# The first 36 microseconds of a two-layer decoder: loads reordered, the first gain spread by TensorE, and the engines' order written by hand

## Chip, cores and metric

The kernel runs on one NeuronCore of a Trainium2 chip, as one program. The metric is the device time of a run in microseconds, lower is better. Engines are called by their common names: TensorE (PE, with its weight loads as PEld), VectorE (DVE), ScalarE (ACT), GpSimd (POOL) and SyncE (SP), which here only issues loads.

## What is computed

Two layers over 512 tokens of 1024 features. Only the first step of the first layer matters here: a norm with a gain, and the projection to 416 "latent" columns (256 for queries, 128 for keys and values, 32 rotary) and to the other heads' queries, keys and values.

```python
def rms_norm(x, g):
    xf = x.astype(jnp.float32)
    y = xf * lax.rsqrt(jnp.mean(xf * xf, axis=-1, keepdims=True) + NORM_EPS)
    return (y * g.astype(jnp.float32)).astype(x.dtype)

h = rms_norm(x, ev_pre_g[0])
c_q, c_kv, k_rope, dq, dk, dv = split_cols(h @ ev_w_in[0], EVEN_SPLITS)   # 256, 128, 32, 512, 512, 512
q = heads_first(rms_norm(c_q, cq_g) @ w_uq, MLA_HEADS)
kv = heads_first(rms_norm(c_kv, ckv_g) @ w_ukv, MLA_HEADS)
```

## The kernel before

The 512 tokens are four tiles `X[i]` of 128 partitions by 1024, handled in the order 3, 2, 1, 0 (`ORDER`). Matrix products are done in three parts with split operands: a float32 value is cast to a shorter form `h` on ACT, DVE takes the remainder `l = x - h`, and TensorE adds `h*h`, `h*l` and `l*h` (`mm3`, lines 263 to 265). The class `Weights` does this for weights: `load` issues a load into one of three `wraw` buffers, `split` (lines 72 and 73) casts to `wh` and subtracts to `wl`, and `ahead(n)` sees that n units are made. A load into a `wraw` buffer waits until the split that read it is done. All loads go through SP's queue in program order.

At the start TensorE multiplies a tile of zeros 16 times (`warm`, line 137). The gain `ev_pre_g` is loaded with its row repeated into all 128 partitions. For each token tile, `normalise` computes the mean square on ACT (`Square`, line 188), the reciprocal root on POOL (lines 178 and 181), the product with the gain on DVE in two halves (`xn`, line 201), then four TensorE transposes into a bank of PSUM for each half (`tp`, line 211), a cast on ACT (`xh`, line 171) and the remainder on DVE (`xl`, line 172). Between the tiles one more of the four weight units of the latent projection is made (`W.ahead`). The latent projection `ac` follows for each tile: 8 blocks of 128 features with three products each, 416 columns wide, so 24 products a tile and 96 in all; then the latent norm (`ctok`) and its transposes (`tc`). After that the products of the first differential head (`aqk`, 512 wide) begin.

PSUM has eight banks; `bank("a", ...)` hands out three of them in turn. The order of the instructions on each engine is chosen by the scheduler of the language from the program order and its own costs, except in blocks under `tc.manual_schedule`, where the written order holds for the engines it names.

Of the kernel before, what the change touches and what calls it, by code (L numbers as in the profile page):

```python
# [9 lines left out]
F32 = mybir.dt.float32  # L10
# [3 lines left out]
ALU = mybir.AluOpType  # L14
# [3 lines left out]
P = 128  # L18
S = 512
D = 1024  # L20
NT = S // P
KD = D // P
EPS = 1e-6
# [2 lines left out]
NF = FF // P  # L26
HF = NF // 2
LAM_INIT = 0.8 - 0.6 * math.exp(0.0)
WARM = 16
TURN = 4  # L30
ORDER = (3, 2, 1, 0)

# [54 lines left out]
def trunk(tc, A, out):  # L87
    nc = tc.nc
    PE, ACT, DVE, POOL = nc.tensor, nc.scalar, nc.vector, nc.gpsimd

    with ExitStack() as top:
# [36 lines left out]
        def load_x(i):  # L128
            nc.sync.dma_start(X[i][:], A["x"][i * P:(i + 1) * P, :])

        load_x(3)

        zero = chp.tile([P, P], F32, tag="s", name="zero")
        DVE.memset(zero[:], 0.0)
        warm = bank("o", "warm")
        for _ in range(WARM):
            PE.matmul(warm[:, :P], zero[:], zero[:], start=True, stop=True)
        POOL.memset(epst[:], EPS)
        POOL.memset(mhalf[:], -0.5)
# [411 lines left out]
        def even():  # L551
            with ExitStack() as es:
# [3 lines left out]
                dv = ap.tile([P, NT, 512], F32, tag="dv", name="dv")  # L556
                oM = (ap.tile([P, 4, S], F32R, tag="omh", name="omh"),
                      ap.tile([P, 4, S], F32R, tag="oml", name="oml"))
                g_pre = gain("ev_pre_g", 0)
                nc.sync.dma_start(ident[:], A["ident"])  # L560
                for n, i in enumerate(ORDER[1:]):
                    W.load()
                    load_x(i)
                xnT = new_xnT()
                xh, xl = xnT

# [24 lines left out]
                with ExitStack() as e1:  # L591
# [19 lines left out]
                    with ExitStack() as e2:  # L611
# [10 lines left out]
                        nc.sync.dma_start(qtab[:], A["rope_q"])  # L622
                        for i in ORDER:
                            t = slice(i * P, (i + 1) * P)
                            a = bank("a", "ac")
                            for k in range(KD):
# [750 lines left out]
```

## Time and profile before

| | us |
|---|---|
| median of 3 runs | 1167.95 (1167.81 to 1168.21) |
| the profiled execution | 1168.91 |
| its span | 1167.1 |
| TensorE busy | 1145.5, 98% of the span |
| DVE busy | 810.8, 69% |
| ACT busy | 558.2, 48% |

A row of the timeline gives the start in microseconds from the start of the span, the duration, the engine, the source line, the operation, what it writes and reads by the program's names, the shape, how many instructions are merged in it, and in brackets how long the engine was idle before it and what ended that. Products on TensorE are pipelined: the next one starts before the one before it has ended, so the distance between starts is the cost of one. A row of the stretches gives each engine's busy time with the number of instructions, the granted TensorE clock (1.00 is full), the busy share of the DMA engines and the rate.

### The profile page before, as it was taken

To read this page: it belongs to the slowest core of one execution; us is meant where nothing else is said; L and a number is where in the kernel's file an instruction comes from. 1 tells how busy PE (TensorE), PEld (TensorE's weight loads), DVE (VectorE), ACT (ScalarE), POOL (GpSimd) and SP (SyncE) were. 2 spreads that over 40 slices of the span, in tenths; PEclk is the share of its full clock that TensorE was granted. 3 is DMA by queue.
4 is the path that set the end of the run, shared out by engine and by line. 5 is a ranking of instruction groups with operands and counts; after the bars stand their busy time and mean duration, and the time that the engine had idled before them with its cause. 6 is when DMAs were issued, how large, how long until landed. Compare 5 with 4: busy or idle time off the path is not lost. (4 is left out here: it accounts for less than half of the span.)

```text
span 1167.1 us, 15181 instructions
## 1 busy us (share of the span) xinstructions
PE 1145.5 (98%) x5656; PEld 939.4 (80%) x5656; DVE 810.8 (69%) x1424; ACT 558.2 (48%) x942; POOL 57.4 (5%) x138
## 2 busy tenths in 40 slices
PE   8999999999999999999999999999999999999997
PEld 7876667898888888888878877898988888888885
DVE  6677676457766767899863465666676766779896
ACT  5565555245443443457543454544444443445562
POOL 2100012110000000000020000002000000000001
PEclk9999999999999999999999999999999999999999
DMA  8310521043323322355735212322333333324461
GB/s 283 114 63 1 169 73 38 37 138 120 108 91 93 106 90 89 110 154 163 234 114 152 72 55 90 91 74 86 96 112 90 107 92 93 106 81 140 141 207 72
DMA packets 39049, 126.81 MB, mean 109 GB/s; under 512 B 4672, under 2 KB 6336, under 8 KB 38848
## 3 DMA queue, kind: packets, MB, share of 16 engines
q1 hardware_dynamic: 37056, 122.11, 33.6%
q10 hardware_dynamic: 1920, 3.74, 1.1%
q8 instruction: 44, 0.72, 0.3%
q14 instruction: 29, 0.24, 0.1%
HBM read 117.95 MB, written 6.29 MB: 106 GB/s over the span
## 5 line engine op out<-in xcount | busy, mean ns | idle before, releaser
L73 DVE TENSOR_TENSOR wl<-wraw,wh 128x1024 fp32r<-128x1024 f32 (+1 forms) x202 | 244.5, 1218 | 186.2 <-ACT wh L72 185.8
L72 ACT CAST wh<-wraw 128x1024 fp32r<-128x1024 f32 (+1 forms) x202 | 209.7, 1047 | 282.2 <-PE u L264 179.4
L264 PE MATMUL u<-xl,wh 128*128 128x512 f32 (+1 forms) x768 | 285.3, 372 | 0.1
L265 PE MATMUL u<-xh,wl 128*128 128x512 f32 (+1 forms) x768 | 285.2, 372 | 0.0
L263 PE MATMUL u<-xh,wh 128*128 128x512 f32 (+1 forms) x768 | 285.0, 372 | 0.1
L264 PEld LDWEIGHTS u<-xl,wh 128*128 128x128 f32 x768 | 144.6, 188 | 25.3 <-DVE xl L172 0.3
L263 PEld LDWEIGHTS u<-xh,wh 128*128 128x128 f32 x768 | 144.4, 188 | 25.3 <-ACT xh L171 0.6
L265 PEld LDWEIGHTS u<-xh,wl 128*128 128x128 f32 x768 | 144.6, 188 | 25.0
L264 PE MATMUL acc<-wl,gh 128*128 128x512 f32 x248 | 96.5, 389 | 0.0
L265 PE MATMUL acc<-wh,gl 128*128 128x512 f32 x248 | 96.5, 389 | 0.0
L263 PE MATMUL acc<-wh,gh 128*128 128x512 f32 x248 | 96.4, 390 | 0.0
L412 ACT ACTIVATE y<-u,cw 128x512 f32<-128x512 f32 x88 | 67.5, 775 | 1.8 <-PE u L265 1.8
L417 ACT ACTIVATE y<-y 128x512 f32<-128x512 f32 x44 | 27.7, 632 | 85.0 <-DVE y L415 85.0
L415 DVE SCALAR_TENSOR_TENSOR y<-u,cw,y 128x510 f32<-128x510 f32 x88 | 65.6, 747 | 2.5
L413 DVE SCALAR_TENSOR_TENSOR y<-u,cw,y 128x511 f32<-128x511 f32 x88 | 65.1, 744 | 0.9 <-ACT y L412 0.9
L178 POOL TENSOR_TENSOR rv<-ms,epst 128x1 f32<-128x1 f32 x40 | 11.0, 276 | 924.9 <-ACT junk L230 845.1
L263 PEld LDWEIGHTS acc<-wh,gh 128*128 128x128 f32 x248 | 46.5, 188 | 10.2 <-issue 0.5
L265 PEld LDWEIGHTS acc<-wh,gl 128*128 128x128 f32 x248 | 46.6, 188 | 9.7
L264 PEld LDWEIGHTS acc<-wl,gh 128*128 128x128 f32 x248 | 46.5, 188 | 9.6
L263 PE MATMUL apt<-xh,wh 128*128 128x512 f32 x128 | 51.3, 401 | 0.0
L265 PE MATMUL apt<-xh,wl 128*128 128x512 f32 x128 | 50.6, 395 | 0.0
L264 PE MATMUL apt<-xl,wh 128*128 128x512 f32 x128 | 50.5, 395 | 0.0
(297 smaller groups left out, 1907.2 us busy)
## 6 DMA issues: line engine op xcount, KB each, us to landing
wraw<-in_ffn_w_up SPq DMA_DIRECT2D x88, 512.0 KB, 3.6
wraw<-in_ffn_w_down SPq DMA_DIRECT2D x44, 512.0 KB, 3.7
wraw<-in_od_w_dqk SPq DMA_DIRECT2D x12, 512.0 KB, 3.6
wraw<-in_ffn_w_down SPq DMA_DIRECT2D x22, 256.0 KB, 2.7
wraw<-in_ev_w_dqk SPq DMA_DIRECT2D x8, 512.0 KB, 3.6
wraw<-in_ev_w_out SPq DMA_DIRECT2D x8, 512.0 KB, 3.7
spill<-X SPq DMA_DIRECT2D x8, 512.0 KB, 2.6
X<-spill SPq DMA_DIRECT2D x8, 512.0 KB, 6.3
```

The source lines that it names most:

```text
L72: self.nc.scalar.copy(h[:, :w], raw[:, :w])
L73: self.nc.vector.tensor_tensor(l[:, :w], raw[:, :w], h[:, :w].bitcast(F32), ALU.subtract)
L178: POOL.tensor_tensor(v[:, :n], ms, epst[:, :n], ALU.add)
L263: PE.matmul(o, lh, rh, start=first, stop=False, skip_group_check=more)
L264: PE.matmul(o, lh, rl, start=False, stop=False, skip_group_check=more)
L265: PE.matmul(o, ll, rh, start=False, stop=last, skip_group_check=more)
L412: ACT.activation(y[:, z], u, AF.Identity, bias=c[:, 3:4], scale=c[:, 2:3])
L413: DVE.scalar_tensor_tensor(y[:, z, 1:], u[:, :S - 1], c[:, 1:2], y[:, z, 1:], ALU.mult, ALU.add)
L415: DVE.scalar_tensor_tensor(y[:, z, 2:], u[:, :S - 2], c[:, 0:1], y[:, z, 2:], ALU.mult, ALU.add)
L417: ACT.activation(y[:, 0], y[:, 0], AF.Silu)
```

## The change

The loads: the second token tile comes second on SP's queue, then the first weight unit, the identity for the transposes, the second and third weight units, the fourth into a part of `dv` (a buffer that is not used until later), then tiles 1 and 0. The gain's 4 KB row is loaded alone, into partition 0 of a zeroed tile, on ACT's queue.

The gain is spread by two float32 products of a full 128 by 128 tile of ones with that zeroed tile: each row of the result, in two PSUM banks of the tag "a", is the gain. The first two tiles' norms read it there; ACT then copies it back to `g_pre` for the last two.

The order on TensorE, DVE, ACT and POOL is written by hand from the first filler product to tile 0's norm. The fillers are 12 at first, 6 after the gain's products, and one between the two transposes of tile 3. The latent products are issued in groups by kind, and those of tile 2 are issued among those of tile 3.

```diff
-WARM = 16
+WARM = 12
...
-        zero = chp.tile([P, P], F32, tag="s", name="zero")
-        DVE.memset(zero[:], 0.0)
-        warm = bank("o", "warm")
-        for _ in range(WARM):
-            PE.matmul(warm[:, :P], zero[:], zero[:], start=True, stop=True)
...
-                g_pre = gain("ev_pre_g", 0)
+                zero, ones = dqk[0][:, 0, :P], dqk[1][:, 0, :P]
+                POOL.memset(zero, 0.0)
+                g_pre = glob.tile([P, D], F32, tag="gain", name="gain", bufs=2)
+                DVE.memset(g_pre[:], 0.0)
+                POOL.memset(ones, 1.0)
...
+                nc.scalar.dma_start(g_pre[0:1, :], A["ev_pre_g"][0:1, :])
+                load_x(2)
+                W.load()
                 nc.sync.dma_start(ident[:], A["ident"])
-                for n, i in enumerate(ORDER[1:]):
-                    W.load()
-                    load_x(i)
+                W.load()
+                W.load()
+                raw = dv[:, 0:2].rearrange("p a b -> p (a b)")
+                nc.sync.dma_start(raw[:, :832], A["ev_w_c"][3])
+                W.raws.append(raw)
+                load_x(1)
+                load_x(0)
...
-                    for n, i in enumerate(ORDER):
-                        normalise(i, g_pre, xnT, "tn" if i % 2 else "ss")()
-                        W.ahead((2, 3, 4, 4)[n])
+                    first = tc.manual_schedule(engines={PE.engine, DVE.engine, ACT.engine, POOL.engine})
+                    first.__enter__()
...
+                    busy(WARM)
+                    gb = [bank("a", "gb") for _ in range(2)]
+                    for n in range(2):
+                        PE.matmul(gb[n], ones, g_pre[:, n * S:(n + 1) * S], start=True, stop=True)
+                    busy(6)
+                    r3, r2 = mean_square(X[3][:]), mean_square(X[2][:])
+                    xn3 = normed(3, r3, gb)
+                    W.ahead(1)
+                    columns(3, 0, xn3)()
+                    busy(1)
+                    lo = columns(3, 1, xn3)
+                    W.ahead(2)
+                    lo()
+                    W.ahead(3)
+                    xn2 = normed(2, r2, gb)
+                    W.ahead(4)
+                    r1 = mean_square(X[1][:])
...
+                    for ks in ((0, 1), (2, 3), (4, 5)):
+                        for what in ("hh", "lh", "hl") if ks[0] else ("hh", "hl", "lh"):
+                            down_part(3, what, ks)
+                    down_part(3, "hh", (6, 7))
+                    down_part(3, "lh", (6, 7))
+                    for n in range(2):
+                        columns(2, n, xn2)()
+                    for n in range(2):
+                        ACT.copy(g_pre[:, n * S:(n + 1) * S], gb[n])
+                    r0 = mean_square(X[0][:])
+                    down_part(2, "hh", range(4))
+                    down_part(2, "hl", range(4))
+                    down_part(3, "hl", (6, 7))
+                    down_part(2, "lh", range(4))
+                    down_part(2, "hh", range(4, 8))
+                    down_part(2, "hl", range(4, 8))
+                    g_sb = [g_pre[:, :S], g_pre[:, S:]]
+                    xn1 = normed(1, r1, g_sb)
+                    for n in range(2):
+                        columns(1, n, xn1)()
+                    down_part(2, "lh", range(4, 8))
+                    xn0 = normed(0, r0, g_sb)
+                    first.__exit__(None, None, None)
+                    for n in range(2):
+                        columns(0, n, xn0)()
```

`busy(n)` issues n filler products; `normed` is the DVE part of `normalise` in two halves; `columns(i, n, xn)` issues the four transposes and the cast of one half and returns the DVE remainder; `down_part(i, what, ks)` issues the latent products of one kind of tile i for the blocks `ks`, into a bank that it takes from tag "a" at the first of them.

More of the change, by code (lines that the diff above doesn't have):

```diff
@@ L131, in trunk @@
         load_x(3)
-        zero = chp.tile([P, P], F32, tag="s", name="zero")
-        DVE.memset(zero[:], 0.0)
-        warm = bank("o", "warm")
-        for _ in range(WARM):
-            PE.matmul(warm[:, :P], zero[:], zero[:], start=True, stop=True)
-        POOL.memset(epst[:], EPS)
-        POOL.memset(mhalf[:], -0.5)
         def ffn_units(layer):
@@ L558, in even @@
                       ap.tile([P, 4, S], F32R, tag="oml", name="oml"))
-                g_pre = gain("ev_pre_g", 0)
-                nc.sync.dma_start(ident[:], A["ident"])
-                for n, i in enumerate(ORDER[1:]):
-                    W.load()
-                    load_x(i)
+                zero, ones = dqk[0][:, 0, :P], dqk[1][:, 0, :P]
[3 more added lines that the diff above has]
+                POOL.memset(ones, 1.0)
+                POOL.memset(epst[:], EPS)
+                POOL.memset(mhalf[:], -0.5)
+                nc.scalar.dma_start(g_pre[0:1, :], A["ev_pre_g"][0:1, :])
+                load_x(2)
+                W.load()
+                nc.sync.dma_start(ident[:], A["ident"])
+                W.load()
[5 more added lines that the diff above has]
+                load_x(0)
                 xnT = new_xnT()
@@ L595, in even, with busy @@
                     mv = mp.tile([P, NT, 512], F32, tag="mv", name="mv")
-                    for n, i in enumerate(ORDER):
-                        normalise(i, g_pre, xnT, "tn" if i % 2 else "ss")()
-                        W.ahead((2, 3, 4, 4)[n])
+                    first = tc.manual_schedule(engines={PE.engine, DVE.engine, ACT.engine, POOL.engine})
+                    first.__enter__()
+                    warm = bank("o", "warm")
+                    def busy(n):
+                        for _ in range(n):
+                            PE.matmul(warm[:, :P], zero, zero, start=True, stop=True)
@@ new lines, in normed, with columns @@
+                    def normed(i, r, g):
+                        xn = chp.tile([P, D], F32, tag="s", name="xn")
+                        for half in range(2):
+                            c = slice(half * S, half * S + S)
+                            DVE.scalar_tensor_tensor(xn[:, c], X[i][:, c], r[:, 0:1], g[half], ALU.mult, ALU.mult)
+                        return xn
+                    def columns(i, n, xn):
+                        tp = bank(("tn" if i % 2 else "ss")[n], "tp", 4, P)
+                        for k in range(4):
+                            PE.transpose(tp[:, k], xn[:, (4 * n + k) * P:(4 * n + k + 1) * P], ident[:])
+                        d = (slice(None), slice(4 * n, 4 * n + 4), slice(i * P, (i + 1) * P))
+                        ACT.copy(xh[d], tp)
+                        return lambda: DVE.tensor_tensor(xl[d], tp, xh[d].bitcast(F32), ALU.subtract)
@@ new lines, in even, with down_part @@
+                    W.ahead(2)
[4 more added lines that the diff above has]
+                    r1 = mean_square(X[1][:])
+                    ac, done = {}, {}
+                    def down_part(i, what, ks):
+                        if i not in ac:
+                            ac[i], done[i] = bank("a", "ac"), 0
+                        t = slice(i * P, (i + 1) * P)
+                        for k in ks:
+                            c = slice((k % 2) * 416, (k % 2 + 1) * 416)
+                            done[i] += 1
+                            PE.matmul(ac[i][:, :416], (xl if what == "lh" else xh)[:, k, t],
+                                      W.made[k // 2][what == "hl"][:, c], start=done[i] == 1, stop=done[i] == 3 * KD)
@@ L624, in even @@
                             t = slice(i * P, (i + 1) * P)
-                            a = bank("a", "ac")
-                            for k in range(KD):
+                            if i not in ac:
+                                ac[i] = bank("a", "ac")
+                            a = ac[i]
+                            for k in range(KD) if i < 2 else ():
                                 wh, wl = wc[k // 2]
```

## The prediction, made before the changed kernel was run

> **What bounds the kernel now.** I read the page first, then TensorE's timeline over the first 36 us, then the clock and engine shares by stretches of 3.41 us, then ACT, DVE, POOL and the loads in the same stretch. The page:
>
> ```profile
> span 1167.1 us, 15181 instructions
> PE 1145.5 (98%) x5656; PEld 939.4 (80%) x5656; DVE 810.8 (69%) x1424; ACT 558.2 (48%) x942; POOL 57.4 (5%) x138
> ```
>
> TensorE is the bound: a change at the start is worth only what it does to the moment from which TensorE runs without a gap. TensorE's timeline (start, duration, idle before) shows that moment:
>
> ```profile
> 1.05 5.61 PE L137 MATMUL warm<-zero 128*128 128x128 f32 x32 [1.05 <-DVE zero L134]
> 7.73 1.32 PE L211 MATMUL tp<-ident,xn 128*128 128x128 f32 x8 [1.07 <-DVE xn L201]
> 11.09 0.46 PE L263 MATMUL ac<-wh,xh 128*128 128x416 f32 x1 [2.04 <-ACT xh L171]
> 12.31 1.11 PE L211 MATMUL tp<-ident,xn 128*128 128x128 f32 x4 [0.57 <-DVE xn L201]
> 16.14 0.60 PE L211 MATMUL tp<-ident,xn 128*128 128x128 f32 x4
> 16.50 0.44 PE L265 MATMUL ac<-wh,xl 128*128 128x416 f32 x1
> 16.77 0.35 PE L263 MATMUL ac<-wh,xh 128*128 128x416 f32 x1
> 16.96 0.35 PE L265 MATMUL ac<-wh,xl 128*128 128x416 f32 x1
> 35.58 0.39 PE L263 MATMUL aqk<-xh,wh 128*128 128x512 f32 x1
> ```
>
> After the fillers there are three gaps; from 16 us a product starts every 0.19 us (16.77, 16.96), and four transposes take 0.36 us and slow the next product by 0.08, so 0.44. The first `aqk` product, at 35.58, is my finish line: from there on the changed program issues TensorE's products in the same order as before but for one pair of `tc` transposes, and the other engines' orders converge soon after, so I take the difference there as the difference of the whole. The same stretches with the granted clock (the last three figures of a row: PEclk, DMA share, GB/s):
>
> ```profile
> core 0: us, PE busy (x) PEld busy (x) DVE busy (x) ACT busy (x) POOL busy (x), PEclk, DMA share, GB/s
> 1.39:4.80 3.41, 3.41 (x17) 3.41 (x17) 0.00 (x0) 0.97 (x2) 0.00 (x0) 1.00 0.87 270
> 4.80:8.22 3.42, 2.35 (x21) 2.09 (x19) 1.30 (x2) 0.91 (x3) 0.75 (x2) 1.00 0.98 323
> 8.22:11.63 3.41, 1.36 (x8) 0.72 (x6) 1.27 (x3) 2.99 (x6) 0.74 (x2) 1.00 1.03 419
> 11.63:15.04 3.41, 2.84 (x11) 2.65 (x11) 3.41 (x6) 2.26 (x5) 0.00 (x0) 0.50 0.68 275
> 653.34:656.75 3.41, 2.46 (x12) 1.82 (x11) 3.41 (x8) 1.12 (x1) 0.00 (x0) 1.00 0.75 180
> 656.75:660.16 3.41, 3.41 (x9) 2.63 (x9) 2.03 (x5) 2.08 (x2) 0.00 (x0) 0.50 0.35 132
> ```
>
> After a stretch with 1.36 us of TensorE work, the clock is 0.50 for the next 3.41 us; the same follows 2.46 us of work at 653. (The first stretch shows 1.00, but its products run at the slow pace, below.)
>
> **The change, part by part.** *Fillers and the gain.* The rows of the filler, of a float32 product 512 wide, and of what is available for the new small load:
>
> ```profile
> 3.98 0.63 PE L137 MATMUL warm<-zero 128*128 128x128 f32 x2
> 4.20 0.64 PE L137 MATMUL warm<-zero 128*128 128x128 f32 x2
> 5.94 0.50 PE L137 MATMUL warm<-zero 128*128 128x128 f32 x3
> 6.05 0.50 PE L137 MATMUL warm<-zero 128*128 128x128 f32 x3
> 73.73 0.59 PE L687 MATMUL sps<-mk,mq 128*128 128x512 f32 x1
> 73.73 1.02 PE L687 MATMUL sps<-mk,mq 128*128 128x512 f32 x2
> gain<-in_ev_pre_g SPq DMA_DIRECT2D x1, 512.0 KB, 5.6
> ident<-in_ident SPq DMA_DIRECT2D x1, 64.0 KB, 5.3
> on<-ob SPq DMA_DIRECT2D x16, 33.0 KB, 1.9
> ```
>
> A float32 product is two passes. A filler pass takes 0.21 us before 4.8 us and 0.11 after (starts 3.98, 4.20; 5.94, 6.05); a pass 512 wide takes 1.02 - 0.59 = 0.43. So 12 fillers, 24 passes from 1.1: 17 slow ones to 4.8, 7 fast ones to 5.6. The two gain products, four passes: 1.7, to 7.3. Six more fillers: 1.3, to 8.7. These stand ahead of the first transposes in TensorE's written order, so those start at 8.7, not 7.73: this part *loses* 1.0. The zeros now come from POOL; the trace has no such memset there, so I keep the start of 1.1, and a later one costs at most its own delay, half a microsecond I think.
>
> The gain row must be there by 5.6. It is issued on ACT's queue behind DVE's memset of 1024 columns, which the trace does not show; zeroing 128 columns ended at 1.0, so I take an issue at about 2. Landing takes between 1.9 (33 KB in a quiet queue) and 5.3 (ident behind two loads): 3.9 to 7.3. I take the low end's side, under 5.6, because one row on a queue of its own resembles the 1.9 more; the high end costs 1.7. ACT's table load and first Square stand behind that issue, but Square waits for X until 4.45 anyway.
>
> What the broadcast load cost is little: without it DVE could have started when r was ready.
>
> ```profile
> 4.45 1.06 ACT L188 ACTIVATE junk<-X 128x1024 bf16<-128x1024 f32 x1 [2.44 <-DMA X<-in_x]
> 8.11 0.89 ACT L72 CAST wh<-wraw 128x832 fp32r<-128x832 f32 x1 [2.51 <-DMA wraw<-in_ev_w_c]
> 10.47 1.05 ACT L171 CAST xh<-tp 128x512 fp32r<-128x512 f32 x2
> 6.02 0.56 POOL L181 TENSOR_TENSOR rr<-rv,mhalf 128x1 f32<-128x1 f32 x1
> 6.92 1.42 DVE L201 SCALAR_TENSOR_TENSOR xn<-X,rr,gain 128x512 f32<-128x512 f32 x2 [5.93 <-DMA gain<-in_ev_pre_g]
> 9.03 1.03 DVE L73 TENSOR_TENSOR wl<-wraw,wh 128x832 fp32r<-128x832 f32 x1 [0.69 <-ACT wh L72]
> 12.17 1.28 DVE L172 TENSOR_TENSOR xl<-tp,xh 128x512 fp32r<-128x512 f32 x2
> 6.00:13.00 7.00, 3.31 (x19) 2.30 (x19) 3.94 (x6) 3.78 (x6) 1.30 (x3) 0.90 1.02 411
> ```
>
> r ends at 6.58 and DVE starts at 6.92: 0.3. At the 411 GB/s of the last row, 416 KB weights land about 1 us apart; taking the 512 KB broadcast out and the fourth weight into `dv`, X2 (the second tile) lands near 6, the weights near 7, 8.3, 9.3, 10.3 (estimates). None is then waited for.
>
> *The first tiles.* After: xn3 6.7 to 8.2, transposes 8.7 to 9.9 with one filler between. ACT (orders as built): Square of X3 and X2 and cast 0 before 9; xh of the two halves 9.4 to 10.6; casts 1, 2, 3 from 10.5, 0.8 to 0.9 each, to 13.0; Square of X1 to 14.1. DVE: xl of the first half to 10.7, then wl1 only when cast 1 is done (11.5 to 12.5), the second xl to 13.1, wl2 to 14.0, xn2 to 15.4, wl3 to 16.3. TensorE follows these: tile 3's first products at 10.0, waits of 0.3 before `wh1`, 0.3 before `wl1`, 0.4 before `wl2`, the last of 22 products near 15.2, tile 2's eight transposes to 16.2. Then a new wait. Tile 2's accumulator takes the bank of the first gain product, which frees only when ACT has copied it out; that copy stands behind both xh copies of tile 2 on ACT (15.9, 16.4, then 16.9 to 17.5). So TensorE stands 1.4 and goes on at 17.5.
>
> *Where that stands against before*, by counting `tp` and `ac` work up to 17.5 (two answers, first of `ac`, then of `tp`):
>
> ```profile
> 9.50:17.50 8.00, 4.88 (x18) 4.17 (x19) 0.00 (x0) 0.00 (x0) 0.79 0.76 294
> 0.00:9.50 9.50, 1.31 (x8) 0.84 (x8) 0.00 (x0) 0.00 (x0) 1.00 0.81 270
> 9.50:17.50 8.00, 1.71 (x8) 1.22 (x8) 2.07 (x4) 2.23 (x4) 0.79 0.76 294
> 17.50:35.58 18.08, 17.89 (x106) 1.00 0.63 197
> ```
>
> Before: 18 products and 16 transposes. After: 22 and 16. The lead is 4 x 0.19 = 0.8 us. The last row says that before, TensorE had only 0.2 us idle from there to the finish line, so nothing more can be gained there. After, I find small waits: tile 1's low half behind wl4 and tile 3's latent steps on DVE (0.1), xn0 (0.1), the extra `tc` pair ahead of the line (0.3, of no worth later), and `ctok` of tile 1 (0.4, against 0.2 of before). Counting between none and all of it beyond before, 0.0 to 0.7, I take 0.4.
>
> Sum: -0.8 + 0.4 = -0.4 us. Against the profiled execution, 1168.91 us (1.8 around the span), that is 1168.5; that execution lies 0.96 over the median of 1167.95, so the median becomes 1167.5. Without the chosen middle, 1167.1 to 1167.9; with half a microsecond for the estimated landings and copies either way, 1166.6 to 1168.4.
>
> **The clock gate against the skill.** By my steps TensorE works 3.2 of the 3.41 us up to 11.63 and 3.0 up to 15.04, but only 2.2 of those from 15.04 to 18.46: between the 2.35 that the clock survived and the 1.36 that it did not, and below the 2.46 at 653 that it did not. The Trainium skill, "TensorE: Matmul & The Clock Gate", section "What's actually happening", says that the clock halves after an idle window of about 3.4 us, and that the window is free-running. By that rule no stretch of the changed start would lose its clock. The trace disagrees on the first point: its longest gap before the halving is 2.04 us.
>
> **Rivals.**
> 1. One halved stretch, at 18.46 to 21.87, where TensorE has no gap: 3.41 / 2 = 1.7 lost, 1169.2. For it: the 2.46 row. Against: the 2.35 row. Still within the bound.
> 2. Slower: the small gain load. TensorE's written order lets nothing past the gain products, so each microsecond beyond 5.6 delays everything by one. At 7.3 it is 1.7, and the gap of 1.7 then falls into the stretch that decides the clock for 8.22 to 11.63 (1.4 by my steps, since the slow transposes and products there are what all wait for). 1167.5 + 1.7 + 1.4 = 1170.6. It decides from a landing beyond about 6.5.
> 3. Faster: the written order runs without its waits. If casts and splits overlap better than I lined them up, the 0.3 + 0.3 + 0.4 + 1.4 shrink; all gone gives 1167.5 - 2.4 = 1165.1. Against: DVE has work in nearly all of 11.5 to 16.3.
> 4. The broadcast's removal does nothing: as shown it was worth 0.3 at most, and lies inside my sum.
>
> **The numbers.** Forecast 0.50; rival 1, 0.20; rival 2 or a halved stretch beside another delay, 0.17; rival 3, 0.13. A change under 0.2% (2.3 us; 1165.6 to 1170.3), about what a measurement of this kernel can tell from none, holds the first two. Rival 3 is faster (0.13), rival 2 slower (0.17). Rivals 2 and 3 hold more than 2 in 10, so the range reaches to their prices: 1165.1 to 1170.6; the forecast's own is 1166.6 to 1168.4.
>
> **What would show it.** In the profile after: the first `tp` near 8.7 behind fillers; `gb` starting at 5.6 with no wait for a load; a gap over 1 us ahead of tile 2's first `ac` product, ended by ACT's gain copy; `aqk` at 35.2, and PEclk 1.00 throughout the first 36 us. A first `aqk` before 33.2 or after 37.9 makes it wrong; so does a `gb` that waits for its load.

## Result, and the profile after

The changed kernel takes 1170.35 us (median of 22 runs, 1168.31 to 1172.37), the kernel before 1168.12 (22 runs, 1166.89 to 1170.92). The ratio is 1.0014, with a 95% interval of 1.0008 to 1.0019: 1.6 us slower (0.9 to 2.2), where 0.4 faster was forecast. The profiled execution takes 1171.49 us. Its page:

```profile
span 1169.7 us, 15206 instructions
PE 1149.1 (98%) x5666; PEld 939.9 (80%) x5666; DVE 812.2 (69%) x1424; ACT 558.4 (48%) x944; POOL 56.0 (5%) x140
```

TensorE has ten passes more (5666 for 5656), a figure that turns out to matter. TensorE's timeline of the changed kernel over the same stretch:

```profile
1.06 5.27 PE L608 MATMUL warm<-dqk 128*128 128x128 f32 x24 [1.06 <-POOL dqk L553]
6.17 1.96 PE L628 MATMUL gb<-gain,dqk 128*128 128x512 f32 x4
7.96 1.50 PE L608 MATMUL warm<-dqk 128*128 128x128 f32 x12
9.30 0.60 PE L620 MATMUL tp<-ident,xn 128*128 128x128 f32 x4
15.85 1.03 PE L620 MATMUL tp<-ident,xn 128*128 128x128 f32 x8
18.11 1.03 PE L652 MATMUL ac<-wh,xh 128*128 128x416 f32 x4 [1.22 <-ACT gain L663]
35.91 0.39 PE L254 MATMUL aqk<-xh,wh 128*128 128x512 f32 x1
```

Fillers, gain products, six more fillers, the first `tp` at 9.30 (8.7 was forecast), the gap of 1.22 that ACT's gain copy ends (1.4 at 17.5 was forecast), and the finish line at 35.91, against 35.58 before and 35.2 forecast. The clock by stretches, in the columns explained above:

```profile
8.22:11.63 3.41, 3.40 (x27) 3.10 (x26) 2.32 (x3) 1.62 (x3) 0.00 (x0) 1.00 1.04 418
11.63:15.04 3.41, 3.21 (x14) 2.14 (x13) 3.04 (x4) 2.96 (x5) 0.29 (x2) 1.00 0.70 235
15.04:18.46 3.42, 2.20 (x16) 1.91 (x15) 3.13 (x6) 1.97 (x5) 0.45 (x1) 1.00 0.87 230
657.91:661.32 3.41, 3.41 (x9) 2.64 (x10) 2.41 (x6) 1.70 (x2) 0.00 (x0) 0.50 0.46 143
```

The start keeps its clock, the stretch with 2.20 us of work included. (These stretches are cut where the clock of the execution before could change. In this execution the clock rose at 5.96, and the least busy stretch of its own, 16.20 to 19.61, has 2.19 us of work.) One halved stretch is left, at 658, where before had one at 657.

From 35.58 to the end the kernel before takes 1131.5 us; from 35.91 the changed one takes 1133.8. So 0.3 us of the 2.6 between the two spans lie ahead of the finish line, and 2.3 behind it. Two questions follow: what the start is worth, and what happens behind it, where TensorE's program is the same.

### The profile page after: what moved, and what is told of

It reads as the page before. It is cut to its first block, busy times and chain, and to the rows that moved or that the text cites. A ratio compares the mean times of both kernels' runs of the same rounds, so it can differ in the third digit from the quotient of the medians.

```text
span 1169.7 us, 15206 instructions
## 1 busy us (share of the span) xinstructions
PE 1149.1 (98%) x5666; PEld 939.9 (80%) x5666; DVE 812.2 (69%) x1424; ACT 558.4 (48%) x944; POOL 56.0 (5%) x140
```

## Experiments

Three theories: **A**, all of the loss is made at the start; **B**, most of it comes later and varies from run to run; **C**, TensorE's instructions are themselves loaded by DMA in pieces of 16 KB, the ten extra passes shift these loads against the work, and one of them now falls into a weight load.

All runs in one table. "Passes" are TensorE's filler and gain passes ahead of the work. The next three columns are read in one profiled execution; the last column is that execution's halved stretches, by their start. One near 657 costs TensorE 1.6 us, and must be taken off "aqk to end" before rows are compared. The ratio is taken against the kernel before as it ran beside each run; that kernel's median moved between 1167.7 and 1168.5 from batch to batch, so across batches the ratios are the safer comparison.

| run | passes | first tp | first aqk | aqk to end | median | ratio to before, 95% interval | halved at |
|---|---|---|---|---|---|---|---|
| before, as shown | 32 | 7.73 | 35.58 | 1131.5 | 1168.12 | | 11.6, 656.8 |
| after, as shown | 42 | 9.30 | 35.91 | 1133.8 | 1170.35 | 1.0014 [1.0008, 1.0019] | 657.9 |
| e0 before again | 32 | 7.89 | 34.85 | 1130.5 | 1168.63 | 1.0004 [0.9995, 1.0013] | |
| e1 after again | 42 | 9.33 | 35.93 | 1132.1 | 1169.86 | 1.0018 [1.0009, 1.0027] | |
| e2 no second fillers | 30 | 8.10 | 34.88 | 1131.2 | 1167.88 | 1.0004 [0.9995, 1.0013] | |
| e3 copies first | 42 | 9.38 | 35.93 | 1132.3 | 1169.29 | 1.0012 [1.0002, 1.0021] | |
| e4 before, 5 more fillers | 42 | 8.03 | 35.91 | 1132.0 | 1169.71 | 1.0013 [1.0005, 1.0022] | 12.5 |
| e5 fillers in the gap | 40 | 8.74 | 35.91 | 1130.7 | 1168.32 | 1.0 [0.999, 1.001] | |
| e6 no fillers, copies first | 30 | 8.39 | 34.64 | 1132.1 | 1168.18 | 0.9992 [0.9984, 1.0001] | 656.6 |
| e7 loads only | 32 | 9.37 | 34.32 | 1131.5 | 1168.06 | 0.9994 [0.9985, 1.0002] | |
| e8 more fillers in the gap | 52 | 9.27 | 35.87 | 1132.2 | 1170.45 | 1.0019 [1.0011, 1.0028] | 588.4 |
| e9 row first on SP | 26 | 9.49 | 36.06 | 1131.3 | 1168.09 | 0.9999 [0.9991, 1.0008] | until 12.6 |
| e10 before, 2 more fillers | 36 | 7.80 | 36.02 | 1133.1 | 1169.35 | 1.001 [1.0001, 1.0019] | 13.4, 139.7 |
| e11 six fillers moved | 42 | 8.44 | 35.35 | 1134.0 | 1169.49 | 1.0014 [1.0006, 1.0023] | 657.8 |
| e12 two wide fillers | 34 | 9.31 | 35.92 | 1131.2 | 1167.91 | 0.9996 [0.9987, 1.0005] | |
| e13 as e8 | 52 | 9.25 | 35.84 | 1131.9 | 1169.56 (one run) | | |
| e14 loads only, ident early | 32 | 7.78 | 35.69 | 1129.5 | 1168.03 | 0.9997 [0.9987, 1.0008] | 12.2 |
| e15 one row, 12 fillers | 30 | 8.09 | 34.13 | 1130.6 | 1166.60 | 0.9989 [0.998, 0.9997] | 8.7 |
| e16 row on SP, full height | 30 | 9.34 | 34.85 | 1130.7 | 1167.02 | 0.9987 [0.9978, 0.9996] | |
| e17 ident and weight ahead | 30 | 8.28 | 34.62 | 1133.6 | 1166.61 | 0.9986 [0.9976, 0.9996] | 132.6, 658.3 |

With 1.6 taken off for a stretch halved near 590 or 657, the five rows with 42 passes have 1132.0 to 1132.4 from `aqk` to the end, and the others 1129.5 to 1131.9. (e10 and e17 are left aside: they have a stretch halved near 135, whose price was not separated.)

### How far do two executions of one kernel differ? (e0, e1: no edit)

> The kernel before, unchanged, against itself. In the profiles so far the first aqk product starts at 35.58 us before and at 35.91 us after, 0.33 later, while the spans differ by 2.6 us. Theory A (the loss is at the start: fillers, gain products and the copies of the gain stand in TensorE's way, and the clock rises at another moment of each run): this run's ratio is 1.000, and its aqk start is within 0.5 us of 35.6. Theory B (most of the difference lies in stages after the first 36 us and changes from run to run with the clock's half-rate stretches and the loads): this profile too differs from the first one of the same kernel by 1 us or more after aqk.

> The changed kernel, unchanged. Ratio near 1.0014. Theory A: aqk starts at least 0.3 us later than in the kernel before, and the lag after that point is under 1 us. Theory B: aqk again near 35.9 or anywhere within 1 us of it, and the lag behind the kernel before at the end is again over 1 us more than at aqk, gained at other places than in the first profile.

TensorE's timeline of the kernel before, in this second execution, and its stretches, cut at the places where the granted clock could change here (it rose at 7.04):

```profile
7.89 1.32 PE L211 MATMUL tp<-ident,xn 128*128 128x128 f32 x8 [0.16 <-DVE xn L201]
34.85 0.39 PE L263 MATMUL aqk<-xh,wh 128*128 128x512 f32 x1
```

```profile
7.04:10.45 3.41, 2.00 (x14) 1.33 (x13) 2.44 (x3) 1.80 (x2) 0.00 (x0) 1.00 1.03 416
10.45:13.87 3.42, 2.09 (x10) 1.55 (x11) 2.25 (x4) 2.73 (x7) 0.74 (x2) 1.00 1.00 404
```

The same start, without a halved clock: here the borders of the clock's stretches cut its gaps so that none holds under 2.00 us of work, while in the first execution one held 1.36. The finish line comes at 34.85 for 35.58, 0.73 earlier. The changed start repeats to 0.02 (35.91, 35.93). So against a start of before at full clock the change does not gain 0.4 but loses 1.07. Behind the finish line the two executions of before differ by 1.0 (1131.5 and 1130.5), as theory B had it; the halved stretch at 656.8 in the first accounts for that.

A halved start is no rare accident of the kernel before. Of the six traces with the scheduler's order (before, e0, e4, e7, e10, e14) four have a stretch halved between 11 and 17 us, with finish lines at 35.58 to 36.02; the other two are at 34.85 and 34.32. Of the twelve traces with the order written by hand and gain products of full height, none has one there.

### The changed start, part by part (e2 to e7)

e2 takes out the second fillers, e3 has ACT's gain copies ahead of tile 2's casts:

```diff
# e2
-                    busy(6)
# e3
                     for n in range(2):
-                        columns(2, n, xn2)()
-                    for n in range(2):
                         ACT.copy(g_pre[:, n * S:(n + 1) * S], gb[n])
+                    for n in range(2):
+                        columns(2, n, xn2)()
```

> The changed kernel without the six fillers between the gain's products and the first transposes (12 passes of 0.11 us, 1.34 us by the profile after). Theory A: the first transposes start at about 8.0 instead of 9.3 and aqk up to 1.3 us earlier (34.6 to 35.0), the median 0.8 to 1.3 us lower than the changed kernel's; if the clock falls for lack of work before 11.6, half of it is lost again. Theory B: aqk moves but the whole by less than half of that.

> The changed kernel with ACT's two copies of the gain ahead of the second tile's transposes instead of behind its two xh copies. In the profile after, TensorE stands 1.22 us before the second tile's first product, released by the second of these copies at 18.1, while ACT is idle for 1.90 us until 16.49. Theory A: the wait falls to about 0.3 us (xh done near 17.1), aqk at 34.9 to 35.2, median 0.7 to 1.0 us lower than the changed kernel's. Theory B: whole moved by less than half of that.

e2: the first `tp` comes 1.2 earlier, the finish line 1.05 earlier: in the written order those six fillers delay everything behind them, as the prediction's first step had it. The median falls by 2.0 from e1's, about 1 more than the start explains. e3: TensorE's timeline shows that a wait taken away is not time won.

```profile
17.21 1.02 PE L652 MATMUL ac<-wh,xh 128*128 128x416 f32 x4 [0.24 <-ACT xh L622]
24.27 0.46 PE L256 MATMUL ac<-wh,xl 128*128 128x416 f32 x1 [0.64 <-DVE xl L623]
```

The gap of 1.22 at 18.1 shrinks to 0.24, and a new one of 0.64, for DVE's `xl`, opens at 24.27; the finish line stays at 35.93.

e4 is the kernel before with more fillers; e5 the changed kernel with second fillers moved into the gap; e6 is e2 and e3 together.

```diff
# e4
-WARM = 16
+WARM = 21
# e5
-                    busy(6)
...
                     r0 = mean_square(X[0][:])
+                    busy(5)
                     down_part(2, "hh", range(4))
```

> The kernel before with 21 fillers instead of 16: ten more passes of 0.11 us, 1.1 us, in a gap of TensorE of 1.07 us ahead of the first transposes. Nothing else changes. Theory C (instruction fetch): the changed kernel issues ten passes more on TensorE before aqk than the kernel before (42 against 32), so TensorE's 16 KB instruction loads come ten passes, about 2 us, earlier against the work for the rest of the program and meet other weight loads (seen near 1098 us); so here aqk stays within 0.3 us (once a halved stretch is set aside), while aqk to end grows by 1 to 2 us from 1130.5 (or 1129.7 with a halved stretch at 656 taken out), and the median rises by 1 to 2 us to 1169 to 1170. Theory A (start alone): no change, ratio 1.000.

> The changed kernel without the six fillers ahead of the transposes (as in e2, whose median was 1167.88) but with five fillers in TensorE's idle time of over 1 us ahead of the second tile's first product. Theory C: aqk as in e2 (34.9, at most 0.2 later), but ten passes more are issued before aqk than in e2, so aqk to end goes from 1131.2 back to about 1132.2 and the median is about 1 us above e2's. Theory A: as e2, within 0.4 us.

> The changed kernel without the six fillers and with the gain's copies ahead of the second tile's transposes (e2 and e3 together). In e3 the aqk start did not move (35.93) though the copies were earlier. Theory A and C alike: aqk between 34.0 and 34.9; if it stays at 34.9, the wait for the copies is not what bounds the stage. Median at or up to 0.9 us under e2's 1167.9.

e7 is the kernel before with the changed order of weight and tile loads alone:

```diff
                 g_pre = gain("ev_pre_g", 0)
+                load_x(2)
+                W.load()
                 nc.sync.dma_start(ident[:], A["ident"])
-                for n, i in enumerate(ORDER[1:]):
-                    W.load()
-                    load_x(i)
+                W.load()
+                W.load()
+                raw = dv[:, 0:2].rearrange("p a b -> p (a b)")
+                nc.sync.dma_start(raw[:, :832], A["ev_w_c"][3])
+                W.raws.append(raw)
+                load_x(1)
+                load_x(0)
```

> The kernel before with the changed order of loads alone: the second tile second, the fourth weight unit into dv, gain still loaded with its row repeated, all engines' order left to the scheduler, fillers as before (so TensorE's count of passes is the one of the kernel before). Theory A: the first tile's work is no earlier (it waits for r and the gain), the later ones up to 1 us earlier; aqk between 34.0 and 35.0, median 0 to 1 us below the kernel before. Theory C: aqk to end stays at 1129.7 to 1130.5.

e4 speaks against A alone: ten passes added to the *old* program cost 1.3 per thousand, with a finish line 0.33 behind that of before, both halved. C's forecast for it came true in the time; in its trace the late load costs TensorE 0.7 us, and where the rest of its loss lies isn't shown. e5 is the sharper one against A: its finish line is that of e1 (35.91, 35.93) with two passes fewer, and its ratio is 1.0 for 1.0018. But it missed C's forecast too: with ten passes more than e2 it was to have `aqk` near 34.9, 1132.2 behind it, and a median 1 us above e2's. It had 35.91 and 1130.7, no late load, and a median 0.4 above e2's. The loads' order without the rest (e7) gives the earliest finish line yet, 34.32, though its first `tp` waits 1.82 for the late identity; no difference in the median is clear of the noise.

### Which load is late, and why (e8, e10 to e13)

e8 is the changed kernel with five fillers added in the gap, e10 the kernel before with two more, e11 is e2 with six fillers in the gap.

```diff
# e8; e11 is the same with busy(6), on e2
                     r0 = mean_square(X[0][:])
+                    busy(5)
                     down_part(2, "hh", range(4))
# e10
-WARM = 16
+WARM = 18
```

> The changed kernel with five more fillers in TensorE's idle gap ahead of tile 2's first ac product, so that nothing at the start moves and ten more passes run before the first aqk product (52 for 42). Theory C (TensorE's instruction loads fall at other places of its work and one of them meets the weight load at 1095 us): aqk stays at 35.9, the load moves some 2 us earlier against the work, past the weight load, and the stretch from aqk to the end falls from about 1132.2 to about 1131; the median is about 1168.8. Theory A (all of the loss is at the start): as the changed kernel, 1132.2 behind aqk, about 1169.9.

> The kernel before with 18 fillers for 16 (36 passes for 32). Theory A: the first tp waits for X and the gain and not for fillers, so aqk stays between 34.9 and 35.6 and the median within 0.3 us of before's. Theory C: the instruction load at 1095 us comes 0.8 us earlier against the work, on the edge at which the weight load becomes late (2.6 to 3.0 us behind its issue): between 0 and 1 us slower.

> The changed kernel without its six second fillers, and six fillers in TensorE's idle gap ahead of tile 2's first ac product instead: 42 passes as in the changed kernel, with the early start of the run without them. Theory C: aqk near 34.9 to 35.1, but 1132 behind it, since the instruction load meets the weight load at 1095 us again: a median of about 1168.9, half way between. Theory A: as the run without the six fillers, 1131.2 behind aqk, 1167.9.

e11 came as C had it: with the passes back the time is back (1169.49), though the start is half a microsecond earlier than the changed kernel's. e10 lost (1.0 per thousand, interval 0.1 to 1.9) without a late load at 1095. Its trace has a halved stretch at 139.7, but the granted clock of its runs is that of the kernel before (median 0.996 for both), so this doesn't explain the median, and its cause stays open. e8 missed: slower, where C expected faster. e12 keeps every time of the changed start and takes away instructions only, e13 is e8 once more for its trace:

```diff
-                    busy(6)
+                    for _ in range(2):
+                        PE.matmul(warm[:, :400], zero, g_pre[:, :400], start=True, stop=True)
```

> The changed kernel with its six second fillers (12 passes of 0.11 us) replaced by two fillers 400 columns wide (4 passes of about 0.34 us): the same 1.3 us of work, so that the start keeps its times (first tp 9.3, aqk 35.9), but 34 passes for 42, and so every later TensorE instruction load about 1.7 us later against the work. Theory C: the load at about 1097 us starts some 3 us or more behind the issue of the weight load at 1095 us, behind its last packet; the stretch from 1090 us to the end is about 1 us shorter than in the changed kernel, and the median about 1168.8. Theory A (the loss is the 1.1 us of the start and nothing tied to instruction loads): as the changed kernel, 1169.9 to 1170.4.

> The changed kernel with five more fillers in TensorE's gap once more, for its trace: its first trace showed no late weight load, and yet its median was the changed kernel's. Theory C, with instruction loads whose place varies by up to 1.6 us between executions of one kernel (as between the two traces of the changed kernel, 1.0 and 2.6 us behind the issue): the load starts between 1 us ahead of and 1 us behind the issue, and in this second trace the weight load may well be late by 1 us. If it isn't, and the time is still near 1170, the loss lies at another place, which the trace then shows.

e12's start is the changed kernel's (`tp` 9.31, `aqk` 35.92), and its median is 1167.91, not 1170: theory A falls. Compared product by product, TensorE of e1 and e12 is level at the finish line; e1 is up to 0.44 us ahead between 138 and 587 us, level again within 0.1 from 588 to 1114, and 0.97 behind from 1118 on. The DMA view of e1 from 1095.6 to 1101 (40 slices of 0.135 us with the busy share, the instruction queue, and the weight load with its time to landing):

```profile
DMA  0000000909599599976912000020010000000000
q8 instruction: 1, 0.02, 1.1%
wraw<-in_ffn_w_down SPq DMA_DIRECT2D x1, 512.0 KB, 4.7
```

and of e12:

```profile
DMA  0000001966974859986650004000000000000000
q8 instruction: 1, 0.02, 1.1%
wraw<-in_ffn_w_down SPq DMA_DIRECT2D x1, 512.0 KB, 3.4
```

A packet counts in the slice in which it starts. In e12 the load's last 4 KB packets start by 1098.5, and the lone 4 behind them, at 1098.85, is the instruction load. In e1 the instruction load starts at 1098.21, among the packets, and takes 0.99 us; the lone 2 and 1 behind it, at 1099.18 and 1099.61, are the last two 4 KB packets of the weight load. The load lands 1.3 us later. DVE waits for it, first e1, then e12:

```profile
1100.39 0.69 DVE L290 TENSOR_TENSOR hold<-hold,wraw 128x512 f32<-128x512 f32 x1 [1.19 <-DMA wraw<-in_ffn_w_down]
```

```profile
1099.05 0.68 DVE L290 TENSOR_TENSOR hold<-hold,wraw 128x512 f32<-128x512 f32 x1
```

and TensorE, which until then works on weights that were made earlier, feels it 15 us later, where its products start 0.34 apart for 0.22 (e1, then e12):

```profile
1115.62 0.50 PE L254 MATMUL acc<-gh 128*128 128x512 f32 x1 [0.23 <-DVE uu L471]
1115.96 0.39 PE L255 MATMUL acc<-gl,gh 128*128 128x512 f32 x1
```

```profile
1115.15 0.39 PE L254 MATMUL acc<-gh 128*128 128x512 f32 x1
1115.37 0.39 PE L255 MATMUL acc<-gl,gh 128*128 128x512 f32 x1
```

The same load, over the other traces: landing 4.9, 4.7, 4.9, 4.2 and 5.2 us after its issue in after, e1, e3, e4 and e11, all with 42 passes, and 3.3 to 3.7 in the others. Between 1085 and 1140 us TensorE of these five loses 0.7 (e4) to 1.5 us more than TensorE of e12; in the other fourteen traces it loses 0 to 0.6 more. The Trainium skill, "Runtime: NRT & Kernel Launch", section "Instruction fetch mechanics", says that instructions come in 16 KiB blocks over the sequencer's own DMA queue, and that this is mostly hidden. The page of the profile agrees on the size: 44 loads in that queue, 0.72 MB, and 45 in e8 and e13, the two with the most passes. But here the blocks were not hidden from a weight load.

And e8's slowness: in e13, with 52 passes, the load at 1096 is in time, but one of the first FFN at 514.6 is not. The DMA view from 514.5 to 520, e13 and then e12:

```profile
q8 instruction: 1, 0.02, 1.1%
...
wraw<-in_ffn_w_down SPq DMA_DIRECT2D x1, 256.0 KB, 4.8
```

```profile
wraw<-in_ffn_w_down SPq DMA_DIRECT2D x1, 256.0 KB, 2.5
```

An instruction load lies in e13's stretch and none in e12's; the load is 2.3 late, and TensorE loses 2.1 between 533 and 551. In e8's own trace the instruction load lies at the same place and did no harm, so its median isn't explained by its own trace. Nor is the collision certain elsewhere: e10's instruction load too falls among the last packets of the load near 1098, and that load lands in 3.6. Which of the 16 DMA engines moved a packet is not in the traces; that the delay needs an engine with packets left to move is a guess. So C holds for the five traces with 42 passes, with the rule corrected: more passes don't make late loads go away, they move the instruction loads on to other places.

### A better start (e9, e14 to e17)

Why the gain row was late. The changed kernel issues it at 1.96 on ACT's queue (the last two lines are the copies behind the gap of 1.22 ahead of tile 2):

```profile
1.96 0.52 ACTq L559 DMA_DIRECT2D gain<-in_ev_pre_g  x1
...
16.49 1.07 ACT L622 CAST xh<-tp 128x512 fp32r<-128x512 f32 x2 [1.90 <-PE tp L620]
17.45 1.10 ACT L663 COPY gain<-gb 128x512 f32<-128x512 f32 x2
```

By queue, the first row from 2.0 to 5.3, the other two from 5.3 to 5.7 (q1 is SP's queue, q10 ACT's):

```profile
q1 hardware_dynamic: 330, 1.18, 91.2%
...
q1 hardware_dynamic: 49, 0.16, 101.8%
q10 hardware_dynamic: 1, 0.00, 2.5%
```

Its one packet moved only after 5.3 (at 5.44), after SP's queue had kept the engines busy all that time. e9 loads it first on SP's queue and multiplies one partition only, with fewer fillers and the copies first (as in e3). e14 is e7 with the identity left ahead of `load_x(2)`.

```diff
# e9
-WARM = 12
+WARM = 8
...
+        g_row = glob.tile([P, D], F32, tag="gain", name="gain", bufs=2)
+        nc.sync.dma_start(g_row[0:1, :], A["ev_pre_g"][0:1, :])
...
-                DVE.memset(g_pre[:], 0.0)
-                nc.scalar.dma_start(g_pre[0:1, :], A["ev_pre_g"][0:1, :])
...
-                        PE.matmul(gb[n], ones, g_pre[:, n * S:(n + 1) * S], start=True, stop=True)
-                    busy(6)
+                        PE.matmul(gb[n], ones[0:1, :], g_pre[0:1, n * S:(n + 1) * S], start=True, stop=True)
+                    busy(2)
```

> The changed kernel with the gain row as the first load of SP's queue, no memset, the gain products over one partition only, eight fillers ahead of them and two behind (26 passes before the work for 42), and ACT's gain copies ahead of tile 2's xh copies. If the start is what the fillers and the row's landing make it: gb near 4.5, first tp 7.2 to 7.5, aqk 33.6 to 34.0, and a median 1 to 2 us under before's, 1166 to 1167. Theory B (the start hardly decides the whole): about 1168. Theory C: 1131 behind aqk where the weight load at 1095 us isn't met by an instruction load, 1132 where it is.

> The kernel before with the changed order of the weight and tile loads alone, but the identity's load left where it was, behind the gain's. With the identity late, the first tp waited 1.8 us for it and started at 9.4, and the first aqk product stood at 34.3. Here the first tp should start at 7.6 to 8.0, when xn is ready, and aqk at 33.3 to 34.3; theory A: the median falls by as much, to 1167.0 to 1168.0 with before at 1167.7; theory C: 32 passes as before, so no late weight load at 1095 us and 1130.5 to 1131.5 behind aqk.

e14: `tp` at 7.78 as expected, `aqk` at 35.69 with its clock halved from 12.2; no difference in the median. e9: `gb` at 4.77, but the clock rose only at 12.6, and `aqk` came at 36.06. Too few fillers, or the kind of product? e15 is e9 with twelve fillers ahead and none behind; e16 is e6 with the row on SP's queue.

```diff
# e15
-WARM = 8
+WARM = 12
...
-                    busy(2)
# e16
-                nc.scalar.dma_start(g_pre[0:1, :], A["ev_pre_g"][0:1, :])
+                nc.sync.dma_start(g_pre[0:1, :], A["ev_pre_g"][0:1, :])
```

> The run with the gain row first on SP's queue and one-partition gain products, with twelve fillers ahead of the gain products for eight, and none behind them: TensorE works without a gap from 1.1 to the first tp. If the late clock of that run (1.00 only from 12.6 us) came from too few fillers, the clock now rises between 4.3 and 7.2, gb starts near 5.6 to 6.2 and takes 1.7 to 2.0, the first tp is at 7.5 to 8.2, aqk at 33.8 to 34.4, and the median 0.5 to 1 us under before's. If products over one partition don't count as work for the clock, it rises late again (beyond 9 us), with tp near 9 and aqk near 36. Theory C: 28 passes, no late weight load at 1095 us.

> The run without second fillers and with the gain copies ahead, the gain row issued on SP's queue ahead of the second tile for ACT's: the row should no longer wait behind the other loads, so gb starts right behind the fillers, near 5.7, for 6.4; first tp 7.7 to 7.9, aqk 33.9 to 34.3 (34.64 there), 30 passes, no late weight load at 1095 us, 1131 behind aqk. Theory A and C alike: a median 0.5 to 1 us under before's. If the second tile's load, issued 0.8 us later, is waited for instead, aqk stays at 34.6 and the median at before's.

e15 by stretches of its own clock:

```profile
1.80:5.21 3.41, 3.41 (x18) 3.41 (x17) 0.00 (x0) 0.78 (x2) 0.00 (x0) 1.00 0.83 307
5.21:8.62 3.41, 3.21 (x16) 1.80 (x15) 1.43 (x2) 2.57 (x5) 1.49 (x4) 1.00 0.99 357
8.62:12.03 3.41, 3.41 (x14) 3.31 (x14) 2.34 (x4) 2.69 (x6) 0.00 (x0) 0.51 1.04 416
```

(With the filler between tile 3's transposes e15 has 30 passes, for the 28 of its forecast.) The clock halves behind a stretch in which TensorE was busy for 3.21 of 3.41 us. Of these, 1.98 were gain products over one row:

```profile
5.92 1.98 PE L628 MATMUL gb<-gain,dqk 1*128 1x512 f32 x4
```

So it is the kind of product: products over one row did not hold the clock in e15, and in e9, where TensorE had no gap from 1.06 on and worked on them from 4.77 to 8.55, they did not raise it.

The stretch at 653 in the kernel before, halved behind 2.46 us of work, is less clear. Most of its work is products over 64 rows:

```profile
653.02 1.54 PE L1011 MATMUL zp<-sq,sk 64*128 64x384 f32 x6
655.38 0.92 PE L1011 MATMUL zp<-sq,sk 64*128 64x256 f32 x4 [0.82 <-DVE z L1015]
```

But the same stage lost the clock in five traces (before, after, e6, e11, e17, with 2.46 to 2.52 us of work in the stretch) and kept it in five others (e0, e2, e3, e4, e9, with 2.46 or 2.47). Nor does the busy time of full-height products decide alone: 1.59 us of 3.41 kept the clock in e7 (6.66 to 10.07), and 1.84 lost it in e10 (10.01 to 13.42). What does decide isn't shown.

Both e15 and e16 are faster than before, e15 in spite of its halved stretch. In e16 the first `tp` waits for the identity, 1.48 us; e17 loads the identity and the first weight ahead of the second tile, and puts that tile's Square behind tile 3's casts:

```diff
+                nc.sync.dma_start(ident[:], A["ident"])
+                W.load()
                 load_x(2)
-                W.load()
-                nc.sync.dma_start(ident[:], A["ident"])
...
-                    r3, r2 = mean_square(X[3][:]), mean_square(X[2][:])
+                    r3 = mean_square(X[3][:])
...
                     lo = columns(3, 1, xn3)
+                    r2 = mean_square(X[2][:])
```

> The run with the gain row on SP's queue and full-height products, with the identity and the first weight loaded ahead of the second tile, and the second tile's Square behind tile 3's two xh copies on ACT. The 1.48 us that the first tp waited for the identity go: gb near 6.0, tp 7.8 to 8.0, first ac near 9.2 for 10.65, aqk 33.6 to 34.3 for 34.85, about 1131 behind it (30 passes, no late weight load at 1095 us); theory A and C alike: a median 0.5 to 1 us under that run's. If the second tile's Square now holds the casts up, aqk stays near 34.8 and the median as there.

The wait that ended e16's first gap, and what e17 has in its place (TensorE's timelines, e16 first):

```profile
9.34 0.63 PE L620 MATMUL tp<-ident,xn 128*128 128x128 f32 x4 [1.48 <-DMA ident<-in_ident]
```

```profile
8.28 0.66 PE L620 MATMUL tp<-ident,xn 128*128 128x128 f32 x4
12.21 0.65 PE L652 MATMUL ac<-wh,xh 128*128 128x416 f32 x2 [0.97 <-ACT wh L72]
```

The first `tp` is 1.06 earlier, and most of it goes to a wait of 0.97 for the second cast, which ACT's moved Square holds up: 34.62 for 34.85. e15, e16 and e17 are the fastest of all: 1.3 to 1.6 us under before, by their ratios. Which of the three is best is within the noise.

## Why the prediction was wrong

- **The order of the start: right.** Fillers, gain products, fillers and the delayed first `tp`; 1.2 of loss measured for the six fillers (1.3 forecast); the gap ahead of tile 2 (1.22 for 1.4). All came about 0.6 late.
- **The gain row: mis-sized, and it took the lead away.** A landing "under 5.6" was chosen, by likeness with a quiet queue. The packet moved after 5.3 and the row was there at 6.1 to 6.2. In the profiled execution the slow fillers, which lasted until 5.96 for 4.8, hid that; in e1, where the clock rose at 4.3, `gb` waited 0.69 for it and started at 6.20 all the same. It is rival 2's mechanism at a third of its price. At 18.11, where the changed kernel goes on, it had 22 latent products done, as forecast; but in the trace of before the 22nd had begun by then too, so that nothing was left of the lead of 0.8. The small waits behind were sized about right: 0.33 behind at the finish line, 0.4 forecast for them.
- **The count against one execution: incomplete.** "The lead is 4 x 0.19 = 0.8" was counted in an execution of before whose clock was halved from 11.63 to 15.04. At full clock its finish line is 34.85, not 35.58; the forecast 35.2 would have been a loss of 0.35, and the measured loss is 1.07. Both kinds of start are common in that kernel, and the sum had no term for which one the next execution would have.
- **The rest of the program: wrong, and the larger step.** "I take the difference there as the difference of the whole" failed. Between the two profiled executions the lag of the changed kernel's TensorE is 0.3 us at the finish line, 0.9 at 180, 1.6 at 590, 1.35 at 790 and 2.5 from 1118 on. The last 1.2 come with the late weight load at 1097, into which an instruction load fell; e12, with the same start and eight passes fewer, has no late load there and takes 2.0 less by the medians. No rival held this; rival 2 ended on the right side for another reason. The steps between 130 and 790 are no larger than those between two executions of one kernel (e1 and after stand up to 0.9 apart there), and what makes them wasn't traced.
- **The clock:** rival 1's halved stretch at 18.46 did not come; 2.20 us of work held the clock, as it did with 2.00 in e0. The 2.46 row, on which rival 1 rested, lost the clock in only five of the ten traces that have such a stretch. The Trainium skill, "TensorE: Matmul & The Clock Gate", section "What's actually happening", has the clock halve after an idle window and calls the window free-running. The second part the runs bear out, by borders between 4.3 and 7.2 in all but e9; the first they don't, with e15's window that was 94% busy.

e12 is level with before by the median, though its finish line is 1.07 later than e0's. That doesn't make the start's loss vanish: in those two traces, both at full clock in between, the lag grows from 1.07 to 1.7 at the end. The medians hide it because the kernel before loses its clock oftener: a run's granted clock is 0.997 or more in 39 of 144 runs of before, in 23 of 33 of the changed kernel, and in 10 of 12 of e12. Among the runs with a granted clock of 0.998, before takes 1167.2 us (8 runs), e12 1167.9 (10) and the changed kernel 1168.9 (9; at 0.999 it is 1169.4, 6 runs), so that at an equal clock the start costs some 0.7 and the eight passes 1.0 to 1.5. These are coarse figures, from few runs, and the granted clock counts the last microseconds too, where TensorE has ended. Open: the slowness of e8 and e10, most of e4's, and why TensorE of some traces loses up to 0.6 us near 250 us.

## What to carry to other kernels

A change at the start of a long program also shifts the places at which its instructions are loaded: keep the number of instructions when testing an idea (one wide filler for several narrow ones), or take the difference over the whole program in several executions, and don't equate it with a milestone early on. Before counting a lead against a trace, look whether its clock was halved within the counted stretch, since another execution of the same kernel may not have that; and compare runs of equal granted clock as well as medians, since a change can win in the one and lose in the other. A small load on a queue of its own did not overtake the large ones here; put it first on the queue that fills the DMA engines.

## What was not expected of the hardware

- A 16 KB instruction load that started 0.8 to 2.9 us behind the issue of a 512 KB load, among its packets, came with a landing 0.6 to 1.6 us later in five traces, and in one with a 256 KB load 2.3 late; in e10 and e8 such a load did no harm.
- Products over one row did not hold TensorE's clock: 3.21 of 3.41 us busy with 1.98 over one row lost it, while 2.00 us over full height kept it. With one-row gain products and eight fillers the clock rose only at 12.6. Over 64 rows the same stretch of 2.46 us lost the clock in some executions and kept it in others.
- A one-packet load on ACT's queue, issued at 1.96, moved after 5.3, while SP's queue kept the DMA engines at 91%.
